# The first contraction pair of a tuned matmul with RMS norm: B's tiles moved from the hardware load queue to the casting software queue

## Chip, core and metric

One core of a Trainium2 chip runs the kernel. The metric is device time in microseconds, lower is better. Runs that are compared shared a chip and alternated with runs of the kernel before. Ratios are computed as the mean time of one kernel's fast runs over that of the other's of the same rounds, so they are not quite the ratio of the medians quoted beside them. Every time inside an execution is counted from the first instruction of the span.

## The reference

```python
x = np.matmul(a, b)                                  # a, b: 2048 x 2048, fp32
rms = np.sqrt(np.mean(x ** 2, axis=-1, keepdims=True) + eps)
return (gamma * x / rms).astype(np.float32)
```

## The kernel before

The kernel has a head and a body. The head computes the first 512 rows of the product by plain bf16 products: first the left 1024 columns, contraction pair by contraction pair (a pair is 256 of the 2048 contraction indices, two tiles of 128), then the right 1024. B stays in on-chip memory, and the body computes the other 1536 rows by Strassen's seven products.

TensorE needs, for each pair, a 512 x 256 block of A, transposed on TensorE itself, and a 256 x 1024 block of B in bf16. From pair 1 on, both are loaded by GpSimd's software queue, which can cast fp32 to bf16 under way. Pair 0 has its own path: fp32 loads on the hardware queues of SyncE and ScalarE, and casts by VectorE and ScalarE.

```python
nc.sync.dma_start(out=a0f, in_=a[0:HB * P, 0:W2].rearrange("(r p) k -> p r k", p=P))   # pair 0, A
for t in range(2):
    nc.scalar.dma_start(out=b0f[t], in_=b[t * P:(t + 1) * P, 0:HALF])                  # pair 0, B, fp32
...
def load_b(j, kp):                                   # software queue, casts to bf16
    nc.gpsimd.dma_start(out=raw[j][kp],
        in_=b[kp * W2:(kp + 1) * W2, j * HALF:(j + 1) * HALF].rearrange("(t p) n -> p t n", p=P))
def load_head(kp):                                   # A block (early, "ah"), then B block
    nc.gpsimd.dma_start(out=ah(kp), in_=a[0:HB * P, kp * W2:(kp + 1) * W2].rearrange(...))
    load_b(0, kp)
...
for _ in range(11):                                  # warm-up products on zeros
    nc.tensor.matmul(warm_bank, warm[:, 0:P], warm[:, 0:CH], start=True, stop=True)
```

Seven of the eight 128 x 512 results of a half accumulate in PSUM over all pairs. The eighth has no bank of its own: its two products per pair go to the bank that the transposes also use (`tbank`), and are added up outside by ScalarE (first pair) or VectorE. `stream` issues the seven chunks' products and, between them, the next pair's transposes.

```python
for kp in range(KP):
    ...
    before = [lambda: transpose_head(kp + 1)] if kp + 1 < KP else []
    stream(groups1, kp, before, len(groups1) + 5 if kp == 0 else None)
    ...
    stream_in_parts(last1, kp)                       # the eighth chunk
    if kp > 0:
        b_sums(0, kp - 1)
```

In the profile of the kernel before, `a0f` and `b0f` appear as `early`, and B's left tiles as `b_0_77` (pair 0) to `b_7_84`, the right ones as `b_0_85` to `b_7_92`. In the traces of the changed kernel and of the experiments the numbers are left out, so that all of them are `b`.

## Time and profile before

| | before |
|---|---|
| time, median of 4 runs beside the changed kernel | 226.54 us (226.37 to 226.69) |
| span of the profiled run | 224.8 us |
| TensorE busy | 212.1 us, 94% |
| first real product | 7.87 us |
| pair 1 taken up (B landed at) | 12.68 us (12.63) |
| pair 4 taken up (B landed at) | 24.72 us (24.68) |

The head of the page, engine, busy us, share of the span, instructions:

```profile
span 224.8 us, 3025 instructions
...
PE 212.1 (94%) x1043; PEld 98.6 (44%) x1043; DVE 161.8 (72%) x324; ACT 129.4 (58%) x272; POOL 24.5 (11%) x49
```

TensorE is busy 94% of the time. What is left is mostly the start and the end, so the start is where a gain can be.

TensorE's timeline (start us, duration, engine, line, operation, out<-in; in brackets the idle time before it and what ended it):

```profile
...
1.47 4.54 PE L138 MATMUL acc<-sq 128*128 128x512 bf16 x11 [1.47 <-DVE sq L129]
6.72 0.63 PE L148 MATMUL tbank<-identity_f,early 128*128 128x128 f32 x4 [0.72 <-POOL msq L198]
...
7.87 2.92 PE L341 MATMUL acc<-b_0_77,head_at 128*128 128x512 bf16 x12
...
12.02 0.59 PE L373 MATMUL tbank<-b_0_77,head_at 128*128 128x512 bf16 x2 [0.35 <-DVE head_at L170]
12.68 1.67 PE L341 MATMUL acc<-b_1_78,head_at 128*128 128x512 bf16 x7
...
16.57 1.67 PE L341 MATMUL acc<-b_2_79,head_at 128*128 128x512 bf16 x7
...
24.72 1.67 PE L341 MATMUL acc<-b_4_81,head_at 128*128 128x512 bf16 x7 [0.18 <-DMA b_4_81<-in_b_dram]
...
61.47 1.67 PE L341 MATMUL acc<-b_7_92,head_at 128*128 128x512 bf16 x7
```

The warm-up ends at 6.0 us, A is transposed at 6.72 us (the bracket names GpSimd's `msq`, but A itself had landed only at 6.59 us), products start at 7.87 us. From 12.68 us on a pair takes 3.9 us (12.68 to 16.57). There is almost no idle time between pairs, which looks as if TensorE alone set the pace.

The chain that ended last (start, duration, what) says that it does not:

```profile
...
6.63 0.55 POOL early L106
7.18 17.50 DMA b_4_81<-in_b_dram
24.68 0.04 issue
24.72 1.67 PE acc L341 x7
```

The load of b_4 is on the chain from its issue at 7.18 us to its landing at 24.68 us, and only then TensorE takes over. The issue table (out<-in, queue, count, KB written each, us from issue to landing) gives the landings:

```profile
...
early<-in_b_dram ACTq DMA_DIRECT2D x2, 512.0 KB, 6.5
...
early<-in_a_dram SPq DMA_DIRECT2D x1, 512.0 KB, 5.8
b_1_78<-in_b_dram POOLq DMA_DIRECT2D x1, 512.0 KB, 10.5
...
b_4_81<-in_b_dram POOLq DMA_DIRECT2D x1, 512.0 KB, 17.5
```

b_1 was issued at 2.13 us, so it landed at 12.63 us, 0.05 us before TensorE took it up. Loads and TensorE run at the same pace, and the loads are ahead by a hair.

The windows (stretch, its length, busy us of TensorE, its weight loads, VectorE, ScalarE and GpSimd, granted clock, DMA share, GB/s written) show the stream of loads. The DMA share is the summed duration of the transfers that start in the stretch, over 16 engines. The clock stands as 1.00 where there is no record of it, so it says nothing before 5.54 us, when the record begins:

```profile
...
2.00:3.50 1.50, 1.50 (x5) 0.48 (x4) 0.04 (x1) 1.07 (x1) 1.43 (x5) 1.00 0.85 257
3.50:5.00 1.50, 1.50 (x5) 0.60 (x4) 0.33 (x2) 0.00 (x0) 1.50 (x3) 1.00 0.99 317
5.00:6.50 1.50, 1.01 (x4) 0.16 (x2) 0.52 (x1) 0.52 (x1) 1.50 (x7) 1.00 1.08 263
6.50:8.00 1.50, 1.19 (x9) 0.97 (x10) 0.68 (x3) 0.10 (x1) 1.43 (x6) 1.00 0.91 225
8.00:10.00 2.00, 2.00 (x10) 0.79 (x9) 1.24 (x4) 0.62 (x1) 0.00 (x0) 1.00 1.33 211
```

GB/s is counted at the destination. A casting load reads twice what it writes, so 211 GB/s in the last line is more reading than 317 GB/s in the second. The DMA share stands at 0.85 to 1.33: from 2 us on the engines have much in work. Transfers overlap (1.33 in the last line).

### The profile page before, as it was taken

Reading aid. Unit: us, or ns where it says so; the run is one execution under the profiler, and the core shown is the slowest. Engines: PE = TensorE matmul, PEld = TensorE weight load, DVE = VectorE, ACT = ScalarE, POOL = GpSimd, SP = SyncE. Lnnn points to the kernel's source line nnn. Section 1 sums busy time; section 2 is a strip of 40 time slices with the busy share of each in tenths; the row PEclk is TensorE's granted clock in tenths of the full one; section 3 lists DMA queues with packets and bytes.
Section 4 is the critical chain, followed back from the end, with each engine's and each line's share of the span. In section 5 each row is a group of like instructions: output and inputs, shape, how many; then the busy total and the mean of one; then the engine's idle time right before and its main releaser. Section 6 shows DMA issues by size and latency. Waiting matters only on the chain.

```text
span 224.8 us, 3025 instructions
## 1 busy us (share of the span) xinstructions
PE 212.1 (94%) x1043; PEld 98.6 (44%) x1043; DVE 161.8 (72%) x324; ACT 129.4 (58%) x272; POOL 24.5 (11%) x49
## 2 busy tenths in 40 slices
PE   7899999999999999999998999999999999999950
PEld 2445444444444444444443444444444444444430
DVE  1427567983998989965977578957895579687692
ACT  2210003708697895795673987698587874334570
POOL 8524232200000002000020002000200000000000
PEclk9999999999999999999999999999999999999996
DMA  6999999999962499906589369956994694044045
GB/s 190 219 203 209 202 209 210 212 305 284 331 261 117 187 280 280 345 32 169 238 210 391 118 157 241 350 205 169 225 337 187 96 279 187 0 187 191 0 188 187
DMA packets 36176, 47.13 MB, mean 210 GB/s; under 512 B 21952, under 2 KB 26048, under 8 KB 34496
## 3 DMA queue, kind: packets, MB, share of 16 engines
q0 software_dynamic: 9648, 23.33, 41.3%
q1 hardware_dynamic: 26080, 22.29, 32.7%
q10 hardware_dynamic: 432, 1.31, 2.0%
q8 instruction: 8, 0.13, 0.2%
q14 instruction: 8, 0.07, 0.1%
HBM read 34.60 MB, written 16.78 MB: 229 GB/s over the span
## 4 chain that ended last, share of the span: by engine, by line
PE 57%; DMA 14%; issue 12%; DVE 6%; ACT 5%; POOL 3%; DVEq 0%; ACTq 0%; POOLq 0%
PE acc L279 41%; PE acc L341 15%; DMA b_4_81<-in_b_dram 8%; DMA at_even<-head_at 3%; DMA a_865<-in_a_dram 2%; ACT sq L209 2%; ACT sq L291 1%; POOL early L106 1%; ACT head_at L231 1%; PE tbank L373 1%; PE tbank L165 1%; DVE x_95 L331 1%; DVE x_98 L331 1%; DVE x_96 L331 1%; DVE x_102 L331 1%
## 5 line engine op out<-in xcount | busy, mean ns | idle before, releaser
L341 PEld LDWEIGHTS <-head_at 128*128 128x128 bf16 x240 | 22.9, 98 | 26.6 <-issue 1.1
L279 PEld LDWEIGHTS <-s_104 128*128 128x128 f16 x96 | 9.3, 98 | 12.5 <-DVE s_104 L244 1.4
L279 PEld LDWEIGHTS <-head_at 128*128 128x128 f16 x96 | 9.4, 98 | 11.9 <-issue 0.6
L279 PEld LDWEIGHTS <-s_105 128*128 128x128 f16 x96 | 9.4, 98 | 11.3
L279 PEld LDWEIGHTS <-s_103 128*128 128x128 f16 x96 | 9.4, 98 | 11.3
L279 PEld LDWEIGHTS <-at_even 128*128 128x128 f16 x96 | 9.4, 98 | 11.3
L279 PEld LDWEIGHTS <-s_107 128*128 128x128 f16 x96 | 9.4, 98 | 11.3
L384 ACT COPY x_95<-acc 128x512 f32<-128x512 f32 x1 | 0.6, 585 | 23.8 <-PE acc L341 23.8
L279 PEld LDWEIGHTS <-s_106 128*128 128x128 f16 x88 | 8.6, 98 | 10.4
L279 PE MATMUL acc<-t_left,s_103 128*128 128x512 bf16 x48 | 11.3, 379 | 0.0
L279 PE MATMUL acc<-early,s_103 128*128 128x512 bf16 x48 | 11.3, 379 | 0.0
L279 PE MATMUL acc<-early,head_at 128*128 128x512 bf16 x48 | 10.8, 379 | 0.4 <-ACT x_102 L484 0.4
L279 PE MATMUL acc<-early,at_even 128*128 128x512 bf16 x48 | 10.8, 379 | 0.0
L279 PE MATMUL acc<-t_left,at_even 128*128 128x512 bf16 x48 | 10.8, 379 | 0.0
L279 PE MATMUL acc<-t_left,head_at 128*128 128x512 bf16 x48 | 10.8, 379 | 0.0
L379 DVE TENSOR_TENSOR x_98<-tbank,x_98 128x512 f32<-128x512 f32 x7 | 4.8, 692 | 7.6 <-PE tbank L373 7.6
L317 ACT ACTIVATE rms<-tot 128x1 f32<-128x1 f32 x14 | 2.8, 199 | 12.2 <-DVE tot L316 12.2
L217 DVE TENSOR_SCALAR s<-norm 128x1 f32<-128x1 f32 x12 | 1.8, 148 | 10.9 <-ACT norm L212 10.9
L321 DVE RECIPROCAL r<-rms 128x1 f32<-128x1 f32 x16 | 2.6, 164 | 9.5 <-ACT rms L317 8.4
L170 DVE COPY head_at<-tbank 128x1024 bf16<-128x1024 bf16 x7 | 4.8, 692 | 6.2 <-PE tbank L165 6.2
L291 ACT ACTIVATE sq<-x_97 128x512 bf16<-128x512 f32 x8 | 5.0, 628 | 3.5 <-DVE x_97 L599 3.0
L209 ACT ACTIVATE sq<-a_430 128x1024 bf16<-128x1024 f32 x2 | 2.1, 1058 | 7.5 <-DMA a_430<-in_a_dram 7.5
(390 smaller groups left out, 552.6 us busy)
## 6 DMA issues: line engine op xcount, KB each, us to landing
out_dram<-x_99 SPq DMA_DIRECT2D x4, 512.0 KB, 3.5
out_dram<-x_95 SPq DMA_DIRECT2D x4, 512.0 KB, 2.6
out_dram<-x_96 SPq DMA_DIRECT2D x4, 512.0 KB, 3.0
out_dram<-x_100 SPq DMA_DIRECT2D x4, 512.0 KB, 6.0
out_dram<-x_97 SPq DMA_DIRECT2D x4, 512.0 KB, 2.8
out_dram<-x_101 SPq DMA_DIRECT2D x4, 512.0 KB, 3.7
early<-in_a_dram POOLq DMA_DIRECT2D x7, 256.0 KB, 15.2
out_dram<-x_98 SPq DMA_DIRECT2D x3, 512.0 KB, 2.7
```

Of the source, the lines that this page charges most:

```text
L106: nc.gpsimd.dma_start(out=ah(kp), in_=a[0:HB * P, kp * W2:(kp + 1) * W2].rearrange("(r p) k -> p r k", p=P))
L165: nc.tensor.matmul(view[:, t, r, :], ah(kp)[:, r, t * P:(t + 1) * P], identity, is_transpose=True, start=(t == 0 and r == 0), stop=(t == 1 ...
L170: nc.vector.tensor_copy(out=head_at[:, 2 * kp:2 * kp + 2, :, :], in_=view)
L209: nc.scalar.activation(out=junk, in_=a32[mb][:, h * HALF:(h + 1) * HALF], func=ACTF.Square, scale=2.0 ** -8, accum_out=n2[:, h:h + 1])
L231: nc.scalar.activation(out=a16[mb], in_=a32.pop(mb), func=ACTF.Copy, scale=factor.pop(mb))
L279: nc.tensor.matmul(bank, lhsT[:, kp, :], rhs, start=(start and kp == 0), stop=(kp == KP - 1), skip_group_check=not start)
L291: nc.scalar.activation(out=sq[:, 0:CH], in_=src, func=ACTF.Square, scale=inv_sqrt_n, accum_out=msq[mb][:, c:c + 1])
L317: nc.scalar.activation(out=rms, in_=tot, func=ACTF.Sqrt)
L321: nc.vector.reciprocal(out=r, in_=rms)
L331: nc.vector.scalar_tensor_tensor(out=x, in0=x, scalar=r, in1=gamma_sb[:, h * HALF:(h + 1) * HALF], op0=ALU.mult, op1=ALU.mult)
L341: nc.tensor.matmul(bank, head_at[:, kt, r, :], head_rhs(c, kt), start=(kt == 0), stop=(kt == KT - 1))
L379: nc.vector.tensor_tensor(out=x, in0=part, in1=x, op=ALU.add)
```

## The change

The intent: let the first products start earlier. A comes alone on the hardware queue, B is cast by the software queue (no casts on VectorE and ScalarE), three warm-up products go because A is there sooner, and the eighth chunk's products of pair 0 move between its two tiles so that the transposes of pair 1 do not wait for the bank.

```diff
-    b0f = [early[:, 2048 + t * 2048:2048 + (t + 1) * 2048].bitcast(FP32) for t in range(2)]
...
     for t in range(2):
-        nc.scalar.dma_start(out=b0f[t], in_=b[t * P:(t + 1) * P, 0:HALF])
+        nc.gpsimd.dma_start(out=raw[0][0][:, t, :], in_=b[t * P:(t + 1) * P, 0:HALF])
...
-    load_head(1)
     identity_f = consts.tile([P, P], FP32, name="identity_f")
     make_identity(nc, identity_f)
-    for kp in range(2, 4):
+    for kp in range(1, 4):
         load_head(kp)
...
-    for _ in range(11):
+    for _ in range(8):
         nc.tensor.matmul(warm_bank, warm[:, 0:P], warm[:, 0:CH], start=True, stop=True)
...                                              # transpose_first: no casts of b0f any more
+            move = (nc.vector.tensor_copy, nc.scalar.copy)[t]
+            for h in range(2):
+                pair = slice(2 * h, 2 * h + 2)
+                move(out=head_at[:, t, pair, :], in_=view[t][:, pair, :])
...                                              # stream(groups, kp, before, late)
-            if n == (when or len(groups)):
+            if n == len(groups) + late:
                 for work in before:
                     work()
+            if late and n == len(groups):
+                stream_in_parts(last1, kp)
...
-        stream(groups1, kp, before, len(groups1) + 5 if kp == 0 else None)
+        stream(groups1, kp, before, 3 if kp == 0 else 0)
         if kp == KP - 1:
             evict(groups1, (1, 3, 5))
-        stream_in_parts(last1, kp)
         if kp > 0:
+            stream_in_parts(last1, kp)
             b_sums(0, kp - 1)
```

More of the change, by code (lines that the diff above doesn't have):

```diff
@@ L150, in transpose_first @@
         for t in range(2):
-            cast_first = [lambda: nc.vector.tensor_copy(out=raw[0][0][:, t, :CH],
-                                                        in_=b0f[t][:, :CH]),
-                          lambda: nc.scalar.copy(out=raw[0][0][:, t, CH:], in_=b0f[t][:, CH:])]
-            move = [lambda h=h: nc.vector.tensor_copy(
-                out=head_at[:, t, 2 * h:2 * h + 2, :], in_=view[t][:, 2 * h:2 * h + 2, :])
-                for h in range(2)]
-            for work in (cast_first + move if t == 0 else move + cast_first):
-                work()
+            move = (nc.vector.tensor_copy, nc.scalar.copy)[t]
+            for h in range(2):
+                pair = slice(2 * h, 2 * h + 2)
+                move(out=head_at[:, t, pair, :], in_=view[t][:, pair, :])
     def transpose_head(kp):
@@ L353, in load_later, with stream @@
             load_b(1, which) if kind == "b" else load_block(which)
-    def stream(groups, kp, before=(), when=None):
+    def stream(groups, kp, before=(), late=0):
         order = [(g, kt) for kt in (2 * kp, 2 * kp + 1) for g in groups]
```

## The prediction

> **What bounds the kernel now.** TensorE is busy 212.1 of 224.8 us (first table) and, by the windows, 144.1 of 146 us between 66 and 212 us, so only a rigid shift of the start can help. The early part is tied to loads. The chain of waits runs through the load of b_4 from 7.18 to 24.68 us, then along TensorE. The left B tiles land (issue plus time to landing) at 12.63, 16.4, 20.3, 24.68, 28.5, 32.3, 36.2 us; TensorE takes them up at 12.68, 16.57, 20.47, 24.72, 28.62, 32.52, 36.42. One contraction pair costs 3.9 us on both sides, and TensorE rides 0.05 to 0.25 us behind the loads. An earlier start is worth only what the load stream also moves.
>
> **What opens the stream.** DMA records by queue: the hardware loads (A 0.52 MB, B 1.05 MB fp32) occupy 2.0 to about 8.3 us. The software queue, first issued at 1.25 us, moves nothing before 6.75 us and 0.04 MB before 8.0; then about 200 GB/s written (twice that read). A software load issued at 88.8 us shows data 1.5 us later; one issued at 113.5 us only at 116.25, when the hardware queue fell quiet. I read: the software queue waits while hardware loads keep the engines busy. The Trainium skill ("DMA: Bandwidth & Descriptors", Queues, rings and completion order) says queues take turns by packet; this trace agrees only for 6.75 to 8 us.
>
> **What the change does.**
> - B (1.05 MB read) leaves the hardware queue for the software queue, cast: 256 packets of 2 KB at about 100 per us, 2.6 us (estimate from 10 to 11 us).
> - A alone: 512 packets at about 280 per us, from 2.0 to about 4.3 us, landing 4.4 to 4.9 instead of 6.5.
> - B pieces land at about 5.8 and 7.0 us (second 9.0 before).
> - Four casts of B (0.4 to 0.6 us each) vanish; ACT takes two moves out of PSUM.
> - Three warm-up matmuls go (0.43 us each, cold): warm-up ends at 4.9, not 6.0. The clock was granted in full at 5.8 us, so some fp32 transposes now run cold.
> - The eighth chunk's products move between the tiles: the 0.35 us wait for the transposed bank goes.
>
> **Critical path.** Transposes at about 4.95, first move ready about 6.4, first product about 6.5 us (7.87 before). ah(1) follows B: 1.35 us of packets, then b_1 2.5 us, landing about 11.0 instead of 12.63. TensorE, needing 3.9 us from 6.5, waits about half a microsecond for b_1. Then everything keeps its 3.9 us step, about 1.5 us earlier; b_4 lands about 23.1. Nothing later changes order, so 1.5 us of 226.4 remain: 224.9 us, 0.7% less.
>
> Predicted 224.9 us, 224.2 to 226.0. Faster by over 2%: 1%; within: 98%; slower: 1%.
>
> **What shows it right.** Software-queue data from about 4 us; first product near 6.5; b_1 landing near 11.0, b_4 near 23.1; first right-half product near 38.4 (39.87 before); no new wait after 66 us.
>
> **What would make it wrong.** If the software queue's late first data is a start-up cost and not the hardware load, B lands at 8 us or later, and the gain is zero or negative. If B overlaps the A load, the stream gains up to 2 us. If the clock opens later, first products run cold, but the wait for b_1 hides up to 0.5 us. If a later wait on something unmoved absorbs the shift, the chain of waits will name it.

A correction that does not touch its argument: the times that it takes from the DMA records and from the clock record were read from an origin too early, which makes the ones below 0.15 to 0.26 us too large. By the records, the hardware loads began at 1.85 us, the software queue's first data came at 6.58 us, and the clock opened at 5.54 us. The expectations quoted below have a like shift where they speak of packets. The measured figures in this document are right.

## The result, and the profile after

| | before | after |
|---|---|---|
| time, median of 4 runs each | 226.54 us | 227.84 us (227.60 to 228.21) |
| ratio | | 1.0059 (1.0042 to 1.0077) |
| span of the profiled run | 224.8 us | 225.8 us |
| first real product | 7.87 us | 7.00 us |
| pair 1 taken up | 12.68 us | 12.46 us |
| pair 4 taken up | 24.72 us | 24.91 us |
| first right-half product | 39.87 us | 40.06 us |
| last right-half pair taken up | 61.47 us | 62.28 us |

The changed kernel is slower by 0.6%, where 0.7% less had been predicted. The page:

```profile
span 225.8 us, 3015 instructions
...
PE 210.6 (93%) x1040; PEld 98.3 (44%) x1040; DVE 160.4 (71%) x320; ACT 128.9 (57%) x272; POOL 25.6 (11%) x51
```

TensorE works 1.5 us less (three warm-up products of 0.43 us are gone), but the span is 1.0 us longer, so it waits more. About half of that 1.0 us is the head's: its last product began at 69.78 us before and at 70.23 after. Most of the rest is in two waits of the body, near 112 and 120 us (0.36 and 0.96 us before, 0.47 and 1.26 after). The second is 1.22 and 1.29 us also with B on the hardware queue (e1 and e12), so the change is not shown to cause it. Its timeline:

```profile
...
1.46 3.24 PE L136 MATMUL acc<-sq 128*128 128x512 bf16 x8 [1.46 <-DVE sq L127]
4.53 0.60 PE L146 MATMUL tbank<-identity_f,early 128*128 128x128 f32 x4
...
7.00 1.67 PE L335 MATMUL acc<-b,head_at 128*128 128x512 bf16 x7 [1.43 <-DMA b<-in_b_dram]
8.51 0.59 PE L369 MATMUL tbank<-b,head_at 128*128 128x512 bf16 x2
...
12.46 1.67 PE L335 MATMUL acc<-b,head_at 128*128 128x512 bf16 x7 [1.03 <-DMA b<-in_b_dram]
...
24.91 1.67 PE L335 MATMUL acc<-b,head_at 128*128 128x512 bf16 x7 [0.59 <-DMA b<-in_b_dram]
...
62.28 1.67 PE L335 MATMUL acc<-b,head_at 128*128 128x512 bf16 x7 [0.46 <-DMA b<-in_b_dram]
```

A was transposed at 4.53 us, 2.2 us earlier than before. The first product could have followed at about 5.6 us, but waited 1.43 us for B. TensorE waited again for pair 1 (1.03 us), pair 4 (0.59 us) and the last right-half pair (0.46 us). The bank's wait of 0.35 us (at 12.02 us before) is gone, as planned, and bought nothing: the start of pair 1 is set by its load. The chain:

```profile
...
1.24 0.48 POOL b L93
...
1.90 6.67 DMA b<-in_b_dram
...
8.86 16.01 DMA b<-in_b_dram
...
25.16 15.76 DMA b<-in_b_dram
...
41.20 21.04 DMA b<-in_b_dram
...
62.28 0.61 PE acc L335 x2
```

Now the chain runs through loads from 1.90 to 62.23 us without TensorE in between. Each of the later ones was issued 0.3 us after the landing before it (8.57 and 8.86 us, for example). The first load on the chain is the second B piece of pair 0: issued at 1.90 us, landed at 8.57 us. The prediction had it land at 7.0. The issue table:

```profile
...
early<-in_a_dram SPq DMA_DIRECT2D x1, 512.0 KB, 3.4
b<-in_b_dram POOLq DMA_DIRECT2D x2, 256.0 KB, 6.2
```

A took 3.4 us instead of 5.8. The two B pieces took 6.2 us (median of the two). The windows:

```profile
...
2.00:3.50 1.50, 1.50 (x5) 0.47 (x4) 0.36 (x2) 0.03 (x1) 1.43 (x4) 1.00 0.98 310
3.50:5.00 1.50, 1.50 (x9) 0.91 (x8) 0.00 (x0) 0.00 (x0) 1.50 (x3) 1.00 0.94 171
5.00:6.50 1.50, 0.57 (x6) 0.43 (x5) 0.76 (x2) 0.65 (x2) 1.50 (x3) 1.00 1.02 121
6.50:8.00 1.50, 1.00 (x5) 0.48 (x5) 0.00 (x0) 0.00 (x0) 1.50 (x7) 1.00 1.05 132
8.00:10.00 2.00, 1.81 (x10) 0.65 (x8) 0.00 (x0) 0.59 (x1) 1.00 (x2) 1.00 1.30 207
```

From 5.0 to 8.0 us, when A had long landed, the software queue alone wrote 121 and 132 GB/s, at a DMA share of 1.02 and 1.05. From 8 us on, the same kind of packets ran at 207 GB/s. So during these 3 us the stream ran at 58 to 64% of its later rate (121/207 and 132/207). Against the kernel before, where the same 1.57 MB of pair 0 came through the hardware queues, nothing was won: by 9 us the DMA records hold 2.05 MB read before and 2.12 MB after, a lead of less than 0.2 us.

The records of single transfers say what is slow. This is counted from the DMA records, B's packets only (4 KB read each), as number / median ns / longest ns by start:

```text
kernel          2-4 us          4-6 us          6-8 us          8-10 us         10-12 us
before          87/159/572      72/159/1002     94/221/474      100/173/173     158/173/173
after           38/173/389      127/173/1984    91/207/508      109/173/173     147/173/173
```

From 8 us on a casting packet takes 173 ns, nearly always. Before that, single packets take up to 1984 ns (VectorE and ScalarE were idle from 6.5 to 8.0 us by the windows, so their work does not explain the slow ones there). The slow stretch is in the kernel before, too, on the hardware queue: I had its trace and did not look at single packets there.

The landing record of a load holds 16 times, one for each DMA engine, and TensorE took b_1 up only after the last of them (12.63 and 12.68 us before). For b_1 (pair 1) in ten of the traces, with the span of the profiled run:

```text
                                       b_1 lands: median engine, last engine (last - first)   span
B on the hardware queue   before            11.89   12.63   (0.83)      224.8
                          e1_undo_b         11.89   12.31   (0.55)      225.0
                          e12_chunk_only    11.96   12.20   (0.41)      225.2
B on the software queue   after             11.74   12.41   (1.02)      225.8
                          e3_after_again    12.37   13.67   (1.76)      225.3
                          e16_after_control 12.77   14.46   (2.82)      226.9
                          e9_keep_warm      12.41   14.13   (2.48)      227.2
                          e13_soft_fp32     13.07   14.30   (2.17)      227.0
no 8 KB spacing, hardware e15_before_pitch  11.12   11.55   (0.72)      223.7
no 8 KB spacing, software e14_pitch_all     11.62   12.51   (1.47)      224.9
```

With B on the hardware queue b_1 lands at 12.2 to 12.6 us, run after run (e8 and e18, not in the table, too). With B on the software queue it lands between 12.4 and 14.5 us, differently in every trace (up to 15.0 in e5), and some engines come out of the first 10 us up to 2.8 us behind others. The loads that follow do not make a lag good: in e16 the last engine was still 2.8 us behind the first near 40 us. The run times spread likewise: in 16 runs the changed kernel took 226.23 to 229.18 us, the kernel before 226.1 to 227.25 us in its runs beside the experiments. The start is not all of it, though: the first trace of the changed kernel has b_1 earlier than the kernel before and still a longer span, in part because single packets stalled later (707 ns at 14.7 us, 1205 ns at 59.4 us).

Slow packets alone do not make the difference between the queues. Counted as the time above a packet's usual duration (173, 159, 60 or 46 ns by size and queue), up to 12 us, they cost each of the 16 engines 1.45 us in the kernel before (e1 1.08, e12 1.26) and 1.33 us in the changed kernel (e3 1.65, e16 1.62). What differs more is how many packets were in work at once between 3.5 and 5.5 us, just after A has landed: on the mean 16.1 before (e1 16.5, e12 16.0), but 14.0 in the changed kernel, 13.7 in e3, 10.5 in e16 and 9.3 in e13. (e2, with 16.1, and e4, with A on the software queue too, are exceptions.) With fewer packets than engines some engines stand idle, which gives a least idle time, from 2.5 to 9 us. Slow and idle time together come to 1.56 to 1.73 us an engine in the three traces with B on the hardware queue (median landing of b_1: 11.89 to 11.96 us), and to 1.63 in the first changed trace (11.74), 2.18 in e3 (12.37), 2.65 in e16 (12.77) and 3.02 in e13 (13.07): the median landing goes with this sum. The records do not name the engine of a packet, so which ones stood idle, and why, is not shown.

### The profile page after: what moved, and what is told of

Same layout as the page of the kernel before. It is cut to its first block, busy times and chain, and to the rows that moved or that the text cites. A ratio compares the mean times of both kernels' runs of the same rounds, so it can differ in the third digit from the quotient of the medians.

```text
span 225.8 us, 3015 instructions
## 1 busy us (share of the span) xinstructions
PE 210.6 (93%) x1040; PEld 98.3 (44%) x1040; DVE 160.4 (71%) x320; ACT 128.9 (57%) x272; POOL 25.6 (11%) x51
## 4 chain that ended last, share of the span: by engine, by line
PE 41%; DMA 34%; issue 12%; DVE 6%; ACT 4%; POOL 1%; DVEq 0%; POOLq 0%; ACTq 0%
PE acc L273 41%; DMA b<-in_b_dram 26%; DMA a<-in_a_dram 4%; DMA at_even<-head_at 4%; DVE x L325 2%; DVE x L596 1%; ACT sq L203 1%; ACT head_at L225 1%; DVE x L599 1%; ACT sq L285 1%; ACT x L380 0%; POOL a L114 0%; DVE s L238 0%; DVE r L315 0%; DVE x L494 0%
## 5 line engine op out<-in xcount | busy, mean ns | idle before, releaser
L273 PE MATMUL acc<-b,s 128*128 128x512 bf16 x376 | 83.4, 379 | 1.3 <-DVE s L238 1.3
L273 PEld LDWEIGHTS <-s 128*128 128x128 f16 x472 | 46.1, 98 | 57.2 <-DVE s L238 1.8
L335 PE MATMUL acc<-b,head_at 128*128 128x512 bf16 x240 | 55.4, 379 | 3.5 <-DMA b<-in_b_dram 3.5
L285 ACT ACTIVATE sq<-x 128x512 bf16<-128x512 f32 x62 | 39.1, 631 | 8.6 <-DVE x L596 3.0
L203 ACT ACTIVATE sq<-a 128x1024 bf16<-128x1024 f32 x24 | 25.4, 1057 | 17.6 <-DMA a<-in_a_dram 17.1
L325 DVE SCALAR_TENSOR_TENSOR x<-x,r,gamma_sb 128x1024 f32<-128x1024 f32 x28 | 34.7, 1282 | 0.8
L225 ACT ACTIVATE head_at<-a,s 128x2048 f16<-128x2048 f32 x10 | 19.9, 1990 | 0.0
L99 POOL DMA_DIRECT2D b<-in_b_dram x15 | 10.6, 707 | 16.1 <-DMA b<-in_b_dram 13.8
L285 ACT ACTIVATION_READ_ACCUMULATOR sq<-x 128x1 f32 x62 | 11.7, 188 | 0.0
L273 PE MATMUL acc<-t_left,s 128*128 128x512 bf16 x48 | 11.3, 379 | 0.0
L273 PE MATMUL acc<-early,s 128*128 128x512 bf16 x48 | 11.3, 379 | 0.0
```

What stands on the lines that cost most here:

```text
L99: nc.gpsimd.dma_start(out=raw[j][kp], in_=b[kp * W2:(kp + 1) * W2, j * HALF:(j + 1) * HALF].rearrange("(t p) n -> p t n", p=P))
L203: nc.scalar.activation(out=junk, in_=a32[mb][:, h * HALF:(h + 1) * HALF], func=ACTF.Square, scale=2.0 ** -8, accum_out=n2[:, h:h + 1])
L225: nc.scalar.activation(out=a16[mb], in_=a32.pop(mb), func=ACTF.Copy, scale=factor.pop(mb))
L273: nc.tensor.matmul(bank, lhsT[:, kp, :], rhs, start=(start and kp == 0), stop=(kp == KP - 1), skip_group_check=not start)
L285: nc.scalar.activation(out=sq[:, 0:CH], in_=src, func=ACTF.Square, scale=inv_sqrt_n, accum_out=msq[mb][:, c:c + 1])
L325: nc.vector.scalar_tensor_tensor(out=x, in0=x, scalar=r, in1=gamma_sb[:, h * HALF:(h + 1) * HALF], op0=ALU.mult, op1=ALU.mult)
```

## The experiments

e1 to e4 shared a chip, e5 to e8 another, e9 to e16 a third, e18 a fourth. There is no run e17.

### e1_undo_b: B back on the hardware queue, the rest of the change kept

```diff
-        nc.gpsimd.dma_start(out=raw[0][0][:, t, :], in_=b[t * P:(t + 1) * P, 0:HALF])
+        nc.scalar.dma_start(out=b0f[t], in_=b[t * P:(t + 1) * P, 0:HALF])
# load_head(1) before the identity again, and the four casts of b0f again
```

> The changed kernel with B's first pair put back on the hardware queue as fp32 and cast by VectorE and ScalarE; eight warm-up products and the new place of the eighth chunk stay. Theory S (the software path for B is what cost the time: the load stream gains almost nothing in its median, and some engines fall behind): time back at the kernel before, 226.3 to 226.7 us, ratio 1.000 within 0.002, left tile b_4 again taken up near 24.7 us. Rival R (fewer warm-up products, or the chunk's new place, cost the time): stays at 227.5 us or more, ratio 1.005 or more.

Measured: 226.74 us, ratio 1.001 (0.9998 to 1.0022). The changed kernel in the same rounds (e3) had 1.0045. Theory S holds: the software path for B costs the time. The three warm-up products and the chunk's place cost at most 0.2%. (The undo also puts `load_head(1)` back ahead of the identity; no run separates that.) TensorE's timeline shows where the removed bank wait went:

```profile
...
12.35 1.67 PE L341 MATMUL acc<-b,head_at 128*128 128x512 bf16 x7 [0.44 <-DMA b<-in_b_dram]
...
24.97 1.24 PE L341 MATMUL acc<-b,head_at 128*128 128x512 bf16 x5 [0.76 <-DMA b<-in_b_dram]
```

It became a wait for b_1 (0.44 us) and for b_4 (0.76 us).

### e2_pause: no load issues between 4.5 and 7 us

```diff
-    for kp in range(1, 4):
+    load_head(1)
+    wait_for(raw[0][0][:, 1, 0:1])              # GpSimd waits for B's second piece
+    for kp in range(2, 4):
         load_head(kp)
```

> The changed kernel, but after the loads for pair 1 GpSimd waits for the second piece of B before it issues the loads for pairs 2 and 3, so no load is issued between about 4.5 and 7 us. Theory D (packets are slow from 4.3 to 8 us because GpSimd writes load descriptors all the while): 2 KB packets of the software queue go back to 173 ns from 4.6 us on, the second piece lands by 6.8 us instead of 8.8, the stream gains 1 to 1.5 us, time 225.0 to 225.8 us. Rival H (the slow packets come from elsewhere: the memory or the start itself): packets between 5 and 8 us still show medians of 180 to 250 ns and single ones over 400, time within 0.3 us of the changed kernel.

Measured: 229.53 us with the slow run (229.47 without), ratio 1.0119. B's packets between 6 and 8 us had a median of 226 ns and a longest of 922 ns, although GpSimd issued nothing from about 4.5 us until the second piece was there. Theory D falls. The kernel was slower for a reason that I had not expected: the pause left the queue short, and TensorE waited for pair 2 at 17.61 us. The time says nothing on D, the packets do.

### e3_after_again and e16_after_control: the changed kernel again

> The changed kernel unchanged, again. If the single stalls of about 1 us on two engines (near 59 us in its first trace) are chance, this trace has them elsewhere or not at all while the slow stretch from 4.3 to 8 us stays, and the time is again 227.5 to 228.2 us. If they belong to the kernel, they stand within 1 us of the same place.

> The changed kernel unchanged, as a control on this chip: 227.3 to 227.9 us, ratio 1.004 to 1.006, runs spread over about 2 us, slow packets between 4.3 and 8.5 us.

Measured: 227.54 us (ratio 1.0045, 1.0019 to 1.0072) and, on the other chip, 228.14 us (1.0072, 1.0044 to 1.01). The spread of the runs was 2.1 and 2.5 us. The slow stretch was there both times (longest packets 1529 and 1793 ns). e16 was slower than expected (227.3 to 227.9 us, ratio up to 1.006). Late in the head, near 59.5 us, e3 had two more stalled packets (747 and 708 ns). The first trace of the changed kernel has such stalls near 59 us as well (up to 1205 ns), so they are not plainly chance. But they do not belong to the change: with B on the hardware queue, e1 (412 ns) and e12 (571 ns) have smaller ones at 59.2 to 59.4 us. What they are stays open.

### e4_a_soft: A's first load on the software queue too

```diff
-    nc.sync.dma_start(out=a0f, in_=a[0:HB * P, 0:W2].rearrange(...))
+    nc.gpsimd.dma_start(out=a0f, in_=a[0:HB * P, 0:W2].rearrange(...))
```

> The changed kernel with A's first load, too, on the software queue, ahead of B: nothing on the hardware queues at the start. Theory W (the software queue waits while a hardware load keeps the engines busy): its first data at about 2.8 us, 1.5 us after issue. Rival U (the first software load always starts late): first data at 3.5 us or later, as in the changed kernel, or even near 6.8 us as in the kernel before. Time: within 1 us of the changed kernel either way.

Measured: 227.55 us, ratio 1.0049. First data at 2.88 us, 1.6 us after its issue at 1.26 us. In the changed kernel, with A on the hardware queue, it was 2.0 us after issue (1.24 to 3.27 us), in the kernel before, with A and B there, 5.3 us (1.25 to 6.58 us). Theory W has the right direction, and its size in the changed kernel is only 0.4 us. The slow stretch moved with the later start: no packet of B above 205 ns before 5.2 us, and a median of 300 ns from 6 to 8 us.

### e5_one_load: B's first pair in one software load

```diff
-    for t in range(2):
-        nc.gpsimd.dma_start(out=raw[0][0][:, t, :], in_=b[t * P:(t + 1) * P, 0:HALF])
...
+    load_b(0, 0)
```

> The changed kernel with B's first pair in one software load of both tiles, in the form of all later pairs, in place of two pieces. In every run so far the slow packets stand where the second piece moves, and end when it has landed (about 1.6 MB read in all), at 8 to 9 us. Theory P (a load of one 128-row piece behind another is what goes slow): all 2 KB packets near 173 ns, the pair landed by 7.0 us, b_1 by 11.5, time 225.2 to 226.2 us, faster than the changed kernel by 1.3 us or more. Rival T (the slow stretch belongs to the start of the loads, whatever their form): medians of 180 to 300 ns again between 5 and 8 us, the pair landed at 8 us or later, the first product at 8 us or later, time 227.0 to 228.5 us.

Measured: 230.59 us, ratio 1.0165. Theory P falls: longest packets 1742 and 1529 ns from 4 to 8 us, and the pair landed only at 11.1 us. The time is above rival T's range as well. TensorE's timeline shows a second effect:

```profile
...
11.16 3.15 PE L334 MATMUL acc<-b,head_at 128*128 128x512 bf16 x7 [4.87 <-DMA b<-in_b_dram]
```

Seven products took 3.15 us instead of 1.67: the clock, opened at 5.67 us, fell back to half at 9.08 us, when TensorE had been idle since 6.29 us, and stayed there until 15.91 us. The Trainium skill ("TensorE: Matmul & The Clock Gate", What's actually happening) gives a free-running window of 3413 ns for this. The records agree: the clock was open for 3.41 us, then closed for twice that.

### e6_swapped and e7_same_rows: are certain rows slow?

```diff
 # e6
-    for t in range(2):
+    for t in (1, 0):
 # e7, wrong on purpose
-        nc.gpsimd.dma_start(out=raw[0][0][:, t, :], in_=b[t * P:(t + 1) * P, 0:HALF])
+        nc.gpsimd.dma_start(out=raw[0][0][:, t, :], in_=b[0:P, 0:HALF])
```

> The changed kernel with the two pieces of B issued in the other order (rows 128 to 255 first). Theory A (those rows of B are slow to read): the packets from 3.5 to 5 us are slow, and those after 5 us fast. Rival T (place in time or in the sequence): the first piece is fast, the second slow, as in the changed kernel. The first product then waits for both pieces, near 8.5 us; time 227 to 229 us either way.

> The changed kernel with the second piece reading the rows of the first again (a wrong result on purpose: rows 128 to 255 of B are replaced by rows 0 to 127). Theory A (the rows are slow on first reading): packets at 173 ns throughout, second piece landed by 7 us, time about 225.5 to 226.5 us. Rival T: slow packets from 4.5 to 8 us all the same, time 227 to 228.3 us.

Measured: e6 229.0 us (1.0111), e7 228.22 us (1.0068; result wrong, as intended). In both, the packets between 6 and 8 us were slow (medians 242 and 280 ns, longest 584 and 662 ns), also in e7, where they read rows that had just been read. Theory A falls.

### e8_before_one: the kernel before with one hardware load of B

```diff
-    for t in range(2):
-        nc.scalar.dma_start(out=b0f[t], in_=b[t * P:(t + 1) * P, 0:HALF])
+    nc.scalar.dma_start(out=early[:, 2048:6144].bitcast(FP32).rearrange("p (t n) -> p t n", t=2),
+                        in_=b[0:W2, 0:HALF].rearrange("(t p) n -> p t n", p=P))
```

> The kernel before with its two hardware loads of B made one load of both tiles. Theory P: the 4 KB packets stay near 160 ns, B landed near 7 us instead of 9.0, software loads start by 7 us instead of 8, the stream and the end come 0.7 to 1.2 us earlier: 225.2 to 225.9 us, ratio 0.995 to 0.998. Rival T: slow packets between 4.5 and 8 us as before; both tiles land at about 8.5 us, the first product comes at about 9 us, time 226.3 to 227.5 us.

Measured: 230.35 us, ratio 1.0164, slower than either theory said. With both hardware queues busy to the end, A, too, landed only at 9.1 us, TensorE was idle for 3.0 us, and the clock fell back from 9.37 to 12.78 us. b_1 landed at 12.56 us, as in the kernel before. So in the kernel before the gap between B's two hardware loads is of use: A gets through in it (223 of A's 512 packets start there between 4.5 and 5.5 us, beside 7 of B's).

### e9_keep_warm: eight more warm-up products behind the first transposes

```diff
+        for _ in range(8):
+            nc.tensor.matmul(warm_bank, warm[:, 0:P], warm[:, 0:CH], start=True, stop=True)
         for t in range(2):
             move = (nc.vector.tensor_copy, nc.scalar.copy)[t]
```

> The changed kernel with eight more warm-up products behind the transposes of the first pair, so that TensorE is not idle between about 5.6 and 7.4 us. Theory C (in part of the changed kernel's runs TensorE's clock falls back to half speed while it waits for B, and the first products then run slowly; the runs with a mean granted clock below 0.987 are about 1 us longer than the others): no run below 0.987, the longest runs vanish, median 226.9 to 227.3 us, spread of the runs under 1 us. Rival N (the clock does not matter; the loads alone set the time): the same median as the changed kernel, 227.5 to 227.9 us, and the same spread of 2 us.

Some runs of the changed kernel had a mean granted clock of 0.975 to 0.986, the kernel before never less than 0.987, and in e16's trace the clock was half from 10.49 to 13.90 us. That made the clock a candidate. Measured: no run below 0.989, and still 227.77 us, ratio 1.0057, runs from 226.92 to 229.01 us. Rival N holds: the falling clock goes with a late B, and keeping it open brings no gain that these runs show. The trace:

```profile
...
6.56 2.33 PE L149 MATMUL acc<-sq 128*128 128x512 bf16 x8
8.86 1.67 PE L337 MATMUL acc<-b,head_at 128*128 128x512 bf16 x7
...
14.18 1.67 PE L337 MATMUL acc<-b,head_at 128*128 128x512 bf16 x6 [0.99 <-DMA b<-in_b_dram]
```

TensorE is filled up to 8.86 us, its products run at full speed, and it still waits for pair 1 until 14.18 us, because in this run b_1 landed at 14.13 us.

### e10_late_start: all loads 4 us later

```diff
+    for _ in range(4):
+        nc.gpsimd.memset(x_slot[7], 0.0)
+    nc.gpsimd.memset(early[:, 0:2], 0.0)         # A's load waits for this write
     nc.sync.dma_start(out=a0f, ...
```

> The changed kernel with every load held back by some microseconds of GpSimd work (about 4 to 8 us). Theory Q (slow packets come with the start of the loads, wherever it lies): 2 KB packets are slow again from about 2.3 to 6 us after the first data. Rival Z (something else on the chip in the first 8 us disturbs the loads): packets of loads that begin after 8 us are at 173 ns throughout, and the pair lands within 3 us of A. The total grows by about the delay.

Measured in one look (one run, state unknown): 230.67 us. A's first data came at 5.89 us instead of 1.86. B's packets from 8 to 10 us had a longest of 994 ns, those from 10 to 12 us a median of 217 ns and a longest of 691 ns; from 12 us on all took 173 ns. Rival Z falls: the slow stretch moves with the start of the loads, and loads that begin after 6 us meet it as well. (Z's second sign was there all the same: the pair landed 2.0 us after A, at 12.35 us.)

### e11_pitch: pair 0 of B read as lines end to end

```diff
-        nc.gpsimd.dma_start(out=raw[0][0][:, t, :], in_=b[t * P:(t + 1) * P, 0:HALF])
+        nc.gpsimd.dma_start(out=raw[0][0][:, t, :],
+                            in_=b[t * 64:(t + 1) * 64, :].rearrange("r (h n) -> (r h) n", h=2))
```

> The changed kernel with each piece of B read from 64 whole rows, two partitions to a row, so that the 128 lines of 4 KB lie end to end in memory and not 8 KB apart (a wrong result on purpose). Theory L[...]: packets near 173 ns from 4.3 to 7 us, second piece landed by 7.2 us, time 225.5 to 226.8 us. Rival Q (any load is slow in that stretch): medians of 180 to 290 ns again, second piece landed at 8.5 us or later, time 227.2 to 228.3 us.

A left half of B is 4 KB out of each 8 KB row, so its lines lie 8 KB apart. Here they lie end to end (same bytes, wrong values). Measured: 227.32 us, ratio 1.0031 (1.0007 to 1.0055). The packets from 6 to 8 us were at 173 ns with a longest of 258 ns (first trace of the changed kernel: 207 and 508). But then pair 1, still with lines 8 KB apart, had a median of 221 ns and a longest of 615 ns from 10 to 12 us, where no trace that starts on time and has the 8 KB spacing throughout has a slow packet. Theory L, that the 8 KB spacing of the lines makes packets slow, is half right: the spacing matters, and here the slow packets stand where the first loads with it are. (The spacing alone is not enough: in e14 and e15, below, the first loads with it come near 36 us, and from 33 to 43 us all their packets took 173 ns.) Single stalls (1339 ns between 4 and 6 us) stayed, and the second piece landed at 9.1 us, so the expectation for its landing was missed, and so was the one for the time.

### e12_chunk_only: only the eighth chunk's new place

```diff
 # the kernel before, with the change's edits to stream and its loop alone
-            if n == (when or len(groups)):
+            if n == len(groups) + late:
...
+            if late and n == len(groups):
+                stream_in_parts(last1, kp)
...
-        stream_in_parts(last1, kp)
         if kp > 0:
+            stream_in_parts(last1, kp)
```

> The kernel before with only the new place of the eighth chunk's first two products; B stays on the hardware queue, eleven warm-up products stay. If the head is bound by the loads, the 0.35 us wait for the transposed bank goes and turns into a wait for b_1 or b_4: ratio 1.000 within 0.0015, 226.3 to 226.8 us. If TensorE's own pace binds: 0.2 to 0.4 us faster.

Measured: 226.85 us, ratio 1.0003 (0.9986 to 1.002). The bank's wait is gone, and b_4's stands in its place:

```profile
...
24.76 1.46 PE L341 MATMUL acc<-b,head_at 128*128 128x512 bf16 x6 [0.64 <-DMA b<-in_b_dram]
```

### e13_soft_fp32: software queue without the cast

```diff
-        nc.gpsimd.dma_start(out=raw[0][0][:, t, :], in_=b[t * P:(t + 1) * P, 0:HALF])
+        nc.gpsimd.dma_start(out=b0f[t], in_=b[t * P:(t + 1) * P, 0:HALF])
# and the four casts of b0f by VectorE and ScalarE, as before
```

> The changed kernel with B's first pair still on the software queue in two pieces, but as fp32, cast by VectorE and ScalarE as in the kernel before. Theory K (the order on the software queue costs the time: everything behind B waits on the engines that lag): like the changed kernel, 227.3 to 227.9 us, spread between the engines at b_1 over 0.9 us. Rival V (the cast inside the load costs it): like the kernel before, 226.4 to 226.9 us.

Measured: 228.68 us, ratio 1.0111, b_1 spread over 2.17 us. Not the cast: without it the software queue is as bad or worse, with single packets of 1628 ns. That it is slower than the changed kernel was not expected; here the first products also wait for the casts, and the granted clock was 0.973 to 0.986 in all runs.

### e14_pitch_all and e15_before_pitch: no 8 KB spacing in either kernel

```diff
 # e14: the changed kernel; e15: the kernel before. Pair 0 as in e11 in both. Wrong on purpose.
-            in_=b[kp * W2:(kp + 1) * W2, j * HALF:(j + 1) * HALF].rearrange("(t p) n -> p t n", p=P))
+            in_=(b[kp * P:(kp + 1) * P, :].rearrange("(t r) (h n) -> (r h) t n", t=2, h=2) if j == 0 else
+                 b[kp * W2:(kp + 1) * W2, j * HALF:(j + 1) * HALF].rearrange("(t p) n -> p t n", p=P)))
```

> The changed kernel with all left-half loads of B reading lines that lie end to end (a wrong result on purpose). Theory L (the slow stretch comes from the 8 KB spacing of the lines, and it eats the predicted gain): no slow stretch before 36 us, b_1 landed by 11.5 us, b_4 taken up near 23.3 us, time 224.8 to 225.8 us, about as predicted. Rival Q (it comes with the start of the loads, and e11 was chance): slow packets again between 4.3 and 9 us or between 10 and 12.5 us, time 227.0 us or more.

> The kernel before with the same change of all left-half loads of B (a wrong result on purpose), the control of e14. Theory L: the slow packets of the hardware queue between 5.5 and 8 us shrink, B landed near 7.5 us, b_4 taken up near 24 us, time 225.7 to 226.3 us, so that the changed kernel with the same lines is faster by 0.3 to 1.0 us. Rival Q: 226.4 to 226.8 us, no different from the kernel before.

On one chip, in the same rounds:

| | lines 8 KB apart | lines end to end |
|---|---|---|
| B on the hardware queue | 226.42 us (before) | 224.95 us (e15), ratio 0.9936 |
| B on the software queue | 228.14 us (e16) | 226.55 us (e14), ratio 1.0005 |

Windows of e15, then e14, then e16:

```profile
...
5.00:6.50 1.50, 0.81 (x4) 0.10 (x1) 0.64 (x1) 0.62 (x1) 1.50 (x7) 1.00 1.10 414
6.50:8.00 1.50, 1.37 (x10) 1.05 (x11) 0.79 (x3) 0.06 (x1) 1.43 (x3) 1.00 1.30 242
```

```profile
...
5.00:6.50 1.50, 1.39 (x9) 1.22 (x8) 0.55 (x2) 0.08 (x1) 1.50 (x3) 1.00 0.90 137
6.50:8.00 1.50, 0.98 (x5) 0.50 (x6) 0.20 (x1) 0.57 (x2) 1.50 (x7) 1.00 1.16 176
```

```profile
...
5.00:6.50 1.50, 1.50 (x9) 1.44 (x8) 0.56 (x2) 0.00 (x0) 1.50 (x3) 1.00 0.62 70
6.50:8.00 1.50, 0.26 (x2) 0.03 (x1) 0.20 (x1) 0.65 (x2) 1.10 (x6) 1.00 0.92 116
```

With end-to-end lines the hardware queues write 414 GB/s from 5.0 to 6.5 us, where the kernel before had 263. On the software queue, 70 and 116 GB/s become 137 and 176. So the spacing costs both kernels about the same, 1.5 and 1.6 us. But the difference between the queues stays at 1.6 us (226.55 - 224.95; 1.7 us with the spacing). My theory L was that the spacing eats the predicted gain, and that the changed kernel would win without it. It falls: two losses add up, and the queue's is the one that the change brought. In e14 b_1 landed at 12.51 us, where L had 11.5, and in e15 the gain was larger than L had. Slow packets do not make the queue's loss here: they cost an engine 0.71 us in e14 and 0.87 us in e15. But between 3.5 and 5.5 us 11.6 packets were in work at once in e14, and 16.7 in e15.

### e18_pairs: a correct kernel with another spacing

```diff
 # B: partition p takes rows 2p and 2p+1 of a pair; A: every second column, in all transposes
-                "(t p) n -> p t n", p=P))
+                "(p t) n -> p t n", t=2))
-                    view[:, t, r, :], ah(kp)[:, r, t * P:(t + 1) * P], identity,
+                    view[:, t, r, :], ah(kp)[:, r, t::2], identity,
# and likewise for b0f, a0f and the blocks of the body
```

> The kernel before, with the contraction order inside each pair changed: partition p takes rows 2p and 2p+1 of B (two neighbouring lines instead of two that are 1 MB apart), and the transposes of A take every second column; the result stays right. If what matters is that lines read one after the other by one engine lie close together: slow packets shrink as in e15, 224.8 to 225.8 us. If what matters is how far apart the lines of different engines lie[...]: no better or worse than the kernel before, 226.3 to 227.5 us.

Measured: correct, 227.58 us, ratio 1.0041 (1.0024 to 1.0057). B's packets from 6 to 8 us: median 172 ns, longest 502 ns, so a little better than in the kernel before, and b_1 landed at 12.28 us. The gain is small, and the strided reads and writes of A may have cost more elsewhere (not measured). No version that is both correct and faster than the kernel before was found.

## Why the prediction was wrong, point by point

- **The loads set the pace of the head, and TensorE rides just behind.** Right. The bank wait that the change removed came back as a wait for b_1 or b_4 (e1, e12), with no gain.
- **The software queue waits while hardware loads keep the engines busy.** The direction is right: data 5.3 us after issue with A and B on the hardware queues, 2.0 us with A alone, 1.6 us with nothing there (e4). I used the Trainium skill there ("DMA: Bandwidth & Descriptors", Queues, rings and completion order: queues take turns by packet). The traces agree with turns only after 6.58 us.
- **A alone lands at 4.4 to 4.9 us.** It landed at 4.0 to 4.2 us wherever it had the hardware queues to itself from the start. Right, a little better.
- **"256 packets of 2 KB at about 100 per us, 2.6 us (estimate from 10 to 11 us)", "B pieces land at about 5.8 and 7.0 us".** This is the step that failed. From first data (3.27 us) to the second landing (8.57 us) it took 5.3 us in the first trace, and the pieces landed at 6.96 and 8.57 us; in e3 at 8.24 and 9.80, in e16 at 9.15 and 10.64. The estimate took a rate from a quiet stretch of the trace and used it in a stretch where the same trace already showed slow packets (5 to 7.5 us, up to 1002 ns for a packet of 159). "What would make it wrong" named a start-up cost of the first data; what came was a prompt first datum, then slow packets and engines without work. So the negative gain that it foretold for late B came about, but for another reason.
- **"ah(1) follows B: 1.35 us of packets, then b_1 2.5 us".** Right in size: in the first trace pair 1's A block landed at 9.89 us, 1.3 us after B, and b_1 2.5 us later, at 12.41 instead of the predicted 11.0: the whole miss of 1.4 us was there when B's second piece landed.
- **"Everything keeps its 3.9 us step, about 1.5 us earlier".** The step held, the 1.5 us were not there. I had also counted with mean rates, where the slowest of 16 engines decides: in the first trace the median engine stayed 0.15 us ahead of the kernel before at b_1, the last engine was 0.22 us ahead, and at b_4 the last engine was 0.19 us behind. So in this trace the slow start cancelled the gain, and stalls later on, with the body's two waits, made the loss; in e16 the start alone made b_1 1.8 us later than before.
- **"No new wait after 66 us".** Right: after 66 us the same waits stand as before, two of them 0.1 and 0.3 us longer, one shorter. The new wait stood earlier: 0.46 us at 62.28 us, for the last right-half pair, which had landed 1.1 us later than before. Of the 0.8 us by which this pair was late, the head's last product kept 0.45 us (a wait of 0.55 us near 67 us shrank to 0.20 us).
- **The clock.** The prediction let some transposes run cold and stopped there. In the first trace they did not: the clock opened at 4.21 us, they began at 4.53 us. That a late B lets the clock close again was missed; e9 shows that this is not what costs the time.

What is shown: B's first pair on the software queue makes the kernel 1.1 to 1.7 us slower than on the hardware queue (medians of the same rounds: 1.30 us at first, 1.13 in e3, 1.72 in e16, 1.60 in e14 against e15), and without the cast it is no better (e13). It is not GpSimd's issuing (e2), nor certain rows (e6, e7), nor two pieces in place of one (e5), nor the warm-up or the chunk's place (e1, e12), nor the clock (e9). What is shown besides: both kernels lose about 1.5 us because the lines of half a row of B lie 8 KB apart (e14, e15), and the loss falls on loads at the start of the stream (e10, e11), not on loads with this spacing near 36 us (e14, e15).

What stays open: why the 16 engines have fewer packets in work after A has landed when B is on the software queue, why its longest stalls are longer (1529 to 1984 ns in the changed kernel's three traces, 715 to 1002 ns in those of the kernel before, e1 and e12), and why the slow packets end after some 6 us. Untested is also a plain rival: with the change one queue fewer has work in the first microseconds. No run put B behind A on one hardware queue, so this is not told apart from the software queue itself.

## What to carry to other kernels

Cost a load at the start of a kernel with packet times from the start of a trace, not with the rate of its steady stretch: here the same packets took 173 ns later on and up to 1984 ns in the first 8 us. Look at when the slowest DMA engine lands, and how far the engines are apart, before moving a load to a queue in which everything else waits behind it. Before taking out a wait on TensorE, see what the next instruction would wait for.

## What the Trainium skill lacked or had wrong

- "DMA: Bandwidth & Descriptors", Queues, rings and completion order: queues are said to take turns by packet. Here the software queue moved nothing for 5.3 us after issue while the hardware queues were busy, against 1.6 us without them (e4). Why is not shown.
- "DMA: Bandwidth & Descriptors", Latency and other measured facts: the pitches in the entry on row pitch start at 512 KiB, for copies of 16 KiB a partition. Here 4 KB lines 8 KB apart cost about 1.5 us against lines end to end (226.42 to 224.95 us); their slow packets stood in the first 8 us, and from 8 us on nearly all took 173 ns.
- No page has the slow start itself: casting packets that take 173 ns later had medians of 207 to 300 ns from 6 to 8 us in the changed kernel, e2 to e4, e6, e7, e9 and e16, and single ones took up to 1984 ns in the first 6 us or so after the first data. Later only single packets were slow.
- No page that I read says how long a lag between the DMA engines lasts when loads follow without a gap: 0.4 to 2.8 us at b_1 in the traces of the table, and still 2.8 us near 40 us in e16.
- No page that I read compares a casting packet with a plain one: 173 ns for 4 KB read and 2 KB written on the software queue, 159 ns for 4 KB read and written.
- "TensorE: Matmul & The Clock Gate", What's actually happening: nothing to mend, the window of 3413 ns agrees (3.41 us open, then closed for one or two windows in e5, e8 and e16).
